# From a dense output product to a 32-expert mixture on one core: the router written anew, its neighbours put in another order

## The chip, the cores and the metric

The kernel runs on one core of one Trainium2 chip. A core has five engines that run side by side, each through its own list of instructions in order: TensorE (PE in the rows; PEld is its weight load), VectorE (DVE), ScalarE (ACT), GpSimd (POOL) and SyncE (SP). Here SP does nothing but issue DMAs, which 16 DMA engines carry out. An instruction waits, where it must, for semaphores of other engines, and everything behind it on its engine waits with it. SBUF is the on-chip memory of 128 partitions, PSUM the small memory into which TensorE writes. The metric is the device time of one execution in microseconds.

## The reference, cut to what matters

One decoder layer over 256 tokens of width 2048, in float32. Two token mixers run on the normalised input; they are merged, multiplied by `w_out` and added to `x`. Then comes the part that matters here:

```python
x = x + mixed @ w_out[l]
...
group_prob = softmax(ht @ wr_group + br_group)             # 4 groups
g_prob, g_idx = lax.top_k(group_prob, 1)
expert_logits = (ht @ wr_expert + br_expert).reshape(n_tok, N_GROUPS, EXPERTS_PER_GROUP)
sel = expert_logits[jnp.arange(n_tok), g_idx[:, 0]]        # the 8 experts of the token's group
top_logit, top_idx = lax.top_k(sel, TOP_K_INNER)           # its 2 best
weights = softmax(top_logit) * g_prob
for e in range(N_EXPERTS):                                 # 32
    hid = silu(ht @ w_gate[e]) * (ht @ w_up[e])
    out = out + gates[:, e:e + 1] * (hid @ w_down[e])
return rms_norm(x + out, norm_final_g)
```

Each expert's three matrices are 12 MiB, all 32 experts 384 MiB, read from HBM once.

## The kernel before, in words

**Stages.** The front end (input projection, the two mixers, their output products) is placed by a planner that has no part in the change. Behind it the code is written out in order: the product with `w_out` (four column blocks `n`, each in eight halves `kh` of two k-tiles, each weight half split into a high and a low part `wh`, `wl`); the router; the loop over 32 experts.

**Slots.** Large tiles of 1 MiB share 18 buffers; `slot(name)` takes one, `free(k)` counts k as given back, `room(k)` asks whether k are left. A buffer's next user waits for the last reader of its last tile. Through the `w_out` product the slots hold: 4 of `mix` (the activations), 2 of `acc` (the residual, addressed by `A`), 4 of `xn` (the normalised input, high and low part), one of `rt` (router weights and scratch), and 7 tiles of expert weights, issued earlier. When the front end's small pools close, four more buffers (`wx`) are there beside the slots (`wt`).

**The expert stream.** `Experts` (`xw`) hands out the 384 weight tiles in order: per expert 8 of gate and up (`mgu`), and 4 of down (`md`). `xw.issue` puts DMAs on SP while there is a buffer; `xw.done` gives back the tile just used and issues the next one, so from some point on a tile's DMA waits for the product that last read its buffer.

**Between the two.** `after(n, pss)` adds block `n` of the `w_out` product to `acc`, squares it for the norm, transposes it (PE, into PSUM), copies the transposes to `rt` (ACT), multiplies them with the router weights into `pl`, and splits the block into `xn`. Then `rr` is the reciprocal root of the mean square and `lg` the 36 logits of each token. The router (`first_max` three times) turns these into `asg`, a 0/1 matrix of tokens by experts; three small products with triangular matrices count the tokens of each expert (`pos`, a token's place among the 32 places of an expert). `gather(b)` makes from `pos` a one-hot `oh` for 8 experts and multiplies it with `xn` in eight steps of eight products; ACT copies each step's result to `xg`. `weights()` computes the gate values `gts`, `gtr`. `spread(q)` makes the one-hots `ohr` for four experts, the gate of each place (`gs`, by tiny products) and the transposed one-hots `ogT`.

**The first expert.** For e = 0 the loop takes one step of `gather(0)` before each of its eight steps `kt` of gate and up products (`gu`), then runs `spread(0)`, then `hd` (Silu on ACT, a product on DVE) and its transposes; then expert 1 begins. For e > 0 the steps follow each other as weights come in, and `down(e - 1)`, the scatter products and the later gathers stand between them.

Nearly all instructions are issued by one recording helper, so their line is L167; tiles tell them apart. L301 is the issue of an expert tile, L333 that of a half of the other weights.

## Time and profile before

| | |
|---|---|
| runs of the kernel before | 1785.33, 1789.11, 1793.22 us; median 1789.11 |
| the profiled execution | 1787.91 us device time, of which the span of its instructions is 1786.1 us |
| busy in the span | PE 81%, DVE 46%, ACT 31%, POOL 2% |
| DMA | 534 MB; 421 GB/s from 860 us on |
| where the stages lie | front end to 701 us, `w_out` to 798 us, router to 811 us, experts to the end |

Times in rows count from the start of the span. In rows of the timeline the columns are start, duration, engine (a q behind it: its queue, which issues DMAs), line, operation, out<-in tiles, shapes, number of instructions, and in brackets the idle time of the engine just before and what ended it. PEclk and the granted clock are shares of TensorE's full 2.4 GHz; 0.50 is 1.2 GHz.

### The profile page before, as it was taken

The numbers are of one execution on the slowest core, as the hardware profiler recorded it, in microseconds if no ns is written. First come the engines' busy times: TensorE is split into PE (matmuls) and PEld (weight loads), VectorE is DVE, ScalarE is ACT, GpSimd is POOL, SyncE is SP. The second block draws the span as 40 slices with busy tenths as digits, with TensorE's granted clock in tenths as the row PEclk, the third lists the DMA queues.
The fourth block names the chain that finished last, engine by engine and source line by source line (L and its number), as shares of the span: only waits on it lengthen the run. The fifth ranks groups of instructions, "written<-read, shape, count | busy, mean of one in ns | idle before, by whom it ended". The sixth has DMA issues, their size and how long they took to land.

```text
span 1786.1 us, 29643 instructions
## 1 busy us (share of the span) xinstructions
PE 1451.9 (81%) x12604; PEld 960.8 (54%) x12604; DVE 821.4 (46%) x1241; ACT 556.5 (31%) x919; POOL 33.6 (2%) x64
## 2 busy tenths in 40 slices
PE   7999999999999999996767776667676776676673
PEld 6989998888988999874323222223121332221120
DVE  6999998889944567442212121212121212121213
ACT  6668556666555344442001000011000110000002
POOL 0000000000100000000000000000000000000000
PEclk9999999999999999997978777798877888777766
DMA  6554463334635478538999999999999999999993
GB/s 232 180 163 133 147 209 107 118 105 158 190 117 177 152 254 331 176 125 330 414 421 421 420 421 421 421 420 421 421 421 421 421 420 421 421 421 420 420 421 149
DMA packets 94953, 534.09 MB, mean 299 GB/s; under 512 B 10528, under 2 KB 10544, under 8 KB 45024
## 3 DMA queue, kind: packets, MB, share of 16 engines
q1 hardware_dynamic: 91792, 522.49, 74.5%
q0 software_dynamic: 3024, 9.64, 1.8%
q8 instruction: 102, 1.67, 0.4%
q14 instruction: 35, 0.29, 0.0%
HBM read 526.82 MB, written 5.28 MB: 298 GB/s over the span
## 4 chain that ended last, share of the span: by engine, by line
DMA 49%; PE 40%; DVE 5%; ACT 3%; issue 2%; SPq 0%; DVEq 0%; ACTq 0%
PE mm L167 23%; DMA wt<-in_mgu_dram 21%; DMA wt<-in_md_dram 12%; DMA wx<-in_mgu_dram 11%; PE s L167 7%; PE sd L167 6%; DMA wx<-in_md_dram 3%; PE gu L167 2%; DVE wl L167 2%; DVE vring L167 1%; PE tr L167 1%; ACT wh L167 1%; PE y L167 1%; DMA x<-in_x_dram 1%; ACT ring L167 1%
## 5 line engine op out<-in xcount | busy, mean ns | idle before, releaser
L167 PE MATMUL mm<-hT,wh 128*128 128x256 f32 x2144 | 397.4, 287 | 5.7 <-ACT sg L167 3.0
L167 PEld LDWEIGHTS mm<-hT,wh 128*128 128x128 f32 x2144 | 330.1, 189 | 21.2 <-issue 9.9
L167 PE MATMUL gu<-wt,xg 128*32 128x256 f32 x2896 | 236.8, 457 | 102.8 <-DMA wt<-in_mgu_dram 94.5
L167 DVE TENSOR_TENSOR wl<-wr,wh 128x1024 fp32r<-128x1024 f32 x213 | 259.1, 1217 | 123.2 <-ACT wh L167 121.4
L167 PE MATMUL mm<-hT,wl 128*128 128x256 f32 x1072 | 302.7, 282 | 0.9 <-DVE wl L167 0.9
L167 ACT CAST wh<-wr 128x1024 fp32r<-128x1024 f32 x213 | 222.2, 1043 | 236.3 <-PE mm L167 150.2
L167 PEld LDWEIGHTS gu<-wt,xg 128*32 128x32 f32 x2896 | 88.8, 125 | 223.6 <-DMA wt<-in_mgu_dram 143.0
L167 PEld LDWEIGHTS mm<-hT,wl 128*128 128x128 f32 x1072 | 202.8, 189 | 1.5 <-DVE wl L167 1.3
L167 DVE TENSOR_TENSOR acc<-acc,sc 128x1024 f32<-128x1024 f32 x128 | 150.5, 1217 | 93.2 <-PE sc L167 93.2
L167 DVE SCALAR_TENSOR_TENSOR hd<-gu,gs,hd 64x256 f32<-64x256 f32 x32 | 15.7, 491 | 320.1 <-ACT hd L167 269.0
L167 DVE SCALAR_TENSOR_TENSOR ys<-y,gs,ys 128x512 fp32r<-128x512 f32 x32 | 24.0, 751 | 272.0 <-ACT ys L167 272.0
L167 PE MATMUL gu<-wx,xg 128*32 128x256 f32 x1200 | 104.7, 482 | 45.6 <-DMA wx<-in_mgu_dram 45.0
L167 ACT ACTIVATE ys<-y,gs 128x512 fp32r<-128x512 f32 x32 | 22.0, 687 | 280.0 <-PE y L167 280.0
L167 ACT ACTIVATE hd<-gu,gs 64x256 f32<-64x256 f32 x32 | 15.0, 468 | 259.5 <-PE gu L167 259.1
L167 PEld LDWEIGHTS gu<-wx,xg 128*32 128x32 f32 x1200 | 37.9, 130 | 99.5 <-DMA wx<-in_mgu_dram 68.7
L167 PE MATMUL sc<-ys,ogT 32*128 32x512 f32 x512 | 55.5, 509 | 28.8 <-DVE acc L167 27.7
L167 ACT ACTIVATE xg<-tr,prm 128x256 f32<-128x256 f32 x64 | 26.9, 471 | 161.2 <-PE tr L167 145.2
L167 ACT CAST ogT<-tr 128x256 fp32r<-128x256 f32 x32 | 11.8, 373 | 160.8 <-PE tr L167 160.7
L167 PEld LDWEIGHTS sc<-ys,ogT 32*128 32x128 f32 x512 | 23.6, 213 | 63.6 <-issue 43.6
L167 PEld LDWEIGHTS tr<-oh,xn 128*128 128x128 f32 x256 | 36.0, 209 | 15.5 <-issue 14.4
L167 PE MATMUL tr<-oh,xn 128*128 128x256 f32 x256 | 42.9, 315 | 1.0 <-DVE oh L167 1.0
L167 DVE TENSOR_TENSOR vring<-s,ring 128x512 f32<-128x512 f32 x64 | 42.4, 683 | 0.1
(462 smaller groups left out, 2042.4 us busy)
## 6 DMA issues: line engine op xcount, KB each, us to landing
wt<-in_mgu_dram SPq DMA_DIRECT2D x181, 1024.0 KB, 19.8
wt<-in_md_dram SPq DMA_DIRECT2D x87, 1024.0 KB, 19.8
wx<-in_mgu_dram SPq DMA_DIRECT2D x75, 1024.0 KB, 19.8
wr<-in_win_dram SPq DMA_DIRECT2D x132, 512.0 KB, 3.6
wx<-in_md_dram SPq DMA_DIRECT2D x41, 1024.0 KB, 19.8
wr<-in_wglu_dram SPq DMA_DIRECT2D x32, 512.0 KB, 3.8
wr<-in_wout_dram SPq DMA_DIRECT2D x32, 512.0 KB, 4.3
wr<-in_wro_dram SPq DMA_DIRECT2D x16, 512.0 KB, 6.7
```

The costliest lines, as they stand in the source:

```text
L167: return self._tl.do(Op(self._k, lambda: f(*a, **k), c, outs, ins, own, fn, name == "dma_start"))
```

## The change

Six things are done, in one edit.

- The router finds the two best experts in every group at once (tiles `x1`, `x2` of 4 by 8, with a new constant `io8`), beside the best group, and picks the group at the end; before, it took the group's logits out first.
- `pos` counts from 1, and is compared with 1 to 32, so that a subtraction falls away.
- The last block of `after` is changed: a dummy square root before it brings ACT's table earlier; one of the two copies to `rt` goes to DVE; the low part of `xn` is made behind the router. Silu's table is likewise asked for in `weights()`.
- Two steps of `gather(0)` come before the first expert's first step, so that each later step gathers one ahead; `spread(0)` makes its one-hots right behind `weights()`, and its products with the identity come after `hd` has been issued.
- The `mix` slots hold four k-tiles each in both parts; in the last block of `w_out` they are given back in two parts and a rest, and three expert tiles are issued in between.
- Six products of constants (`ident` with `iot`) follow the router's products on PE.

```diff
@@ -409,6 +409,8 @@
     pool.iota(jp, pattern=[[1, 128]], base=0, channel_multiplier=-1, allow_small_or_imprecise_dtypes=True)
     iot = cp.tile([128, T], F32, name="iot")
     pool.iota(iot, pattern=[[1, T]], base=0, channel_multiplier=0, allow_small_or_imprecise_dtypes=True)
+    io8 = cp.tile([128, 8, 8], F32, name="io8")
+    pool.iota(io8, pattern=[[0, 8], [1, 8]], base=0, channel_multiplier=0, allow_small_or_imprecise_dtypes=True)
     mask = cp.tile([128, 2, 128], F32, name="mask")
     dve.tensor_scalar(mask[:, 0], jp, 0.0, None, op0=OP.is_gt)
     dve.tensor_scalar(mask[:, 1], jp, 0.0, None, op0=OP.is_ge)
@@ -1177,8 +1179,8 @@
         yield
         while not room(4):
             yield "wait"
-        mh = [[slot("mix", F32R) for _ in range(2)] for _ in range(2)]
-        St["mix"] = lambda k: [t[k // 8][:, (k % 8) * T:(k % 8 + 1) * T] for t in mh]
+        mh = [slot("mix", F32R) for _ in range(4)]
+        St["mix"] = lambda k: [mh[k // 4][:, (k % 4 * 2 + x_) * T:(k % 4 * 2 + x_ + 1) * T] for x_ in range(2)]
         yk = [[t[:, k * T:(k + 1) * T] for t in Y] for k in range(8)]
         def put_mix(j, ps):
@@ -1252,6 +1254,9 @@
         xT = [rt[:, 576 + 512 * i:1088 + 512 * i] for i in range(2)]
         pts = [None, None]
+        if n == 3:
+            act.activation(cst[:, 5:6], cst[:, 0:1], AF.Sqrt)
         for i in range(2):
             a = A(i, n * 512)
             dve.tensor_add(a, a, pss[i])
@@ -1265,7 +1270,10 @@
                 pe.transpose(pts[i][:, j * 128:(j + 1) * 128], A(i, n * 512 + j * 128, 128), ident)
         yield
         for i in range(2):
-            act.copy(xT[i], pts[i])
+            if n == 3 and i == 0:
+                dve.tensor_copy(xT[i], pts[i])
+            else:
+                act.copy(xT[i], pts[i])
         yield
         for i in range(2):
             for j in range(4):
@@ -1274,7 +1282,10 @@
         yield
         for i in range(2):
             cs = slice(n * 512, (n + 1) * 512)
-            split(xn[i][0][:, cs], xn[i][1][:, cs], A(i, n * 512))
+            if n < 3:
+                split(xn[i][0][:, cs], xn[i][1][:, cs], A(i, n * 512))
+            else:
+                act.copy(xn[i][0][:, cs], A(i, n * 512))
     prev = iter(())
     for n in range(4):
@@ -1293,10 +1304,18 @@
                     for x_, y_ in ((0, 0), (0, 1), (1, 0)):
                         pe.matmul(pss[i], lhsT=a[x_], rhs=wk[y_], start=(k == 0 and x_ + y_ == 0),
                                   stop=(k == 15 and x_ == 1))
+            if n == 3 and kh in (3, 5, 7):
+                for _ in range(2 if kh == 3 else 1):
+                    free()
+                    xw.issue(xw.n + 1, 2 if kh == 7 else 0)
         prev = after(n, pss)
     for _ in range(4):
         next(prev)
-    free(4)
+    ps = psd()
+    for _ in range(6):
+        pe.matmul(ps[:, :T], lhsT=ident, rhs=iot, start=True, stop=True)
     rr = cp.tile([128, 2, 1], F32, name="rr")
     dve.tensor_reduce(rr, ssp, axis=AX.X, op=OP.add)
     act.activation(rr, rr, AF.Sqrt, bias=c_rms, scale=1.0 / D)
@@ -1325,50 +1344,49 @@
     R = lambda n, w: stile([128, 2] + list(w), "ro_" + n, 1)
     bc = lambda ap, *w: ap.to_broadcast([128, 2] + list(w))
-    def first_max(src, w, nm):
-
-        m = R(nm + "m", [1])
-        dve.tensor_reduce(m, src, axis=AX.X, op=OP.max)
-        eq = R(nm + "e", [w])
-        dve.tensor_tensor(eq, src, bc(m, w), op=OP.is_lt)
-
-        dve.scalar_tensor_tensor(eq, eq, 100.0, bc(iot[:, None, 0:w], w), op0=OP.mult, op1=OP.add)
-        ix = R(nm + "i", [1])
-        dve.tensor_reduce(ix, eq, axis=AX.X, op=OP.min)
-        oh = R(nm + "o", [w])
-        dve.tensor_tensor(oh, bc(iot[:, None, 0:w], w), bc(ix, w), op=OP.is_equal)
-        return m, oh
-
     l4 = lg[:, :, 0:4]
     l32 = lg[:, :, 4:36].rearrange("p i (g e) -> p i g e", g=4)
-    gm, goh = first_max(l4, 4, "g")
-    g48 = bc(goh[:, :, :, None], 4, 8)
+    i4, i48 = bc(iot[:, None, 0:4], 4), io8.rearrange("p (i g) e -> p i g e", i=2)
+    gm, m1, m2 = R("gm", [1]), R("m1", [4]), R("m2", [4])
+    xg_, x1, x2 = R("xg", [4]), R("x1", [4, 8]), R("x2", [4, 8])
+    gi, j1, j2 = R("gi", [1]), R("j1", [4]), R("j2", [4])
+    goh, oh1, oh2 = R("goh", [4]), R("oh1", [4, 8]), R("oh2", [4, 8])
+    e8 = lambda ap: bc(ap[:, :, :, None], 4, 8)
+    dve.tensor_reduce(m1, l32, axis=AX.X, op=OP.max)
+    dve.tensor_reduce(gm, l4, axis=AX.X, op=OP.max)
+    dve.tensor_tensor(x1, l32, e8(m1), op=OP.is_lt)
+    dve.tensor_tensor(xg_, l4, bc(gm, 4), op=OP.is_lt)
+    dve.scalar_tensor_tensor(x1, x1, 100.0, i48, op0=OP.mult, op1=OP.add)
+    dve.scalar_tensor_tensor(xg_, xg_, 100.0, i4, op0=OP.mult, op1=OP.add)
+    dve.tensor_reduce(j1, x1, axis=AX.X, op=OP.min)
+    dve.tensor_reduce(gi, xg_, axis=AX.X, op=OP.min)
+    dve.tensor_tensor(oh1, i48, e8(j1), op=OP.is_equal)
+    dve.tensor_tensor(goh, i4, bc(gi, 4), op=OP.is_equal)
+    sel2 = x1
+    dve.scalar_tensor_tensor(sel2, oh1, -1e30, l32, op0=OP.mult, op1=OP.add)
     ge = R("ge", [4])
     dve.tensor_sub(ge, l4, bc(gm, 4))
     act.activation(ge, ge, AF.Exp)
-    selp = R("selp", [4, 8])
-    dve.tensor_mul(selp, l32, g48)
-    sel = R("sel", [8])
-    dve.tensor_reduce(sel, selp.rearrange("p i g e -> p i e g"), axis=AX.X, op=OP.add)
-    m1, oh1 = first_max(sel, 8, "a")
-    sel2 = R("sel2", [8])
-    dve.scalar_tensor_tensor(sel2, oh1, -1e30, sel, op0=OP.mult, op1=OP.add)
-    m2, oh2 = first_max(sel2, 8, "b")
-    e2 = R("e2", [1])
-    dve.tensor_sub(e2, m2, m1)
-    act.activation(e2, e2, AF.Exp)
-    ohs = R("ohs", [8])
+    dve.tensor_reduce(m2, sel2, axis=AX.X, op=OP.max)
+    dve.tensor_tensor(x2, sel2, e8(m2), op=OP.is_lt)
+    dve.scalar_tensor_tensor(x2, x2, 100.0, i48, op0=OP.mult, op1=OP.add)
+    dve.tensor_reduce(j2, x2, axis=AX.X, op=OP.min)
+    dve.tensor_tensor(oh2, i48, e8(j2), op=OP.is_equal)
+    ohs = x2
     dve.tensor_add(ohs, oh1, oh2)
     asg = R("asg", [32])
-    dve.tensor_mul(asg.rearrange("p i (g e) -> p i g e", g=4), bc(ohs[:, :, None, :], 4, 8), g48)
+    dve.tensor_mul(asg.rearrange("p i (g e) -> p i g e", g=4), ohs, e8(goh))
     pp = pst("tr", 2)
     pe.matmul(pp[:, 0:32], lhsT=mask[:, 0], rhs=asg[:, 0], start=True, stop=True)
     pe.matmul(pp[:, 32:64], lhsT=onesm, rhs=asg[:, 0], start=True, stop=False)
     pe.matmul(pp[:, 32:64], lhsT=mask[:, 0], rhs=asg[:, 1], start=False, stop=True)
+    for i in range(2):
+        dve.tensor_tensor(xn[i][1][:, 1536:], A(i, 1536), xn[i][0].bitcast(F32)[:, 1536:], op=OP.subtract)
     pos = R("pos", [32])
     dve.scalar_tensor_tensor(pos, pp[:, 0:64].rearrange("p (i e) -> p i e", i=2), 1.0, asg, op0=OP.add, op1=OP.mult)
-    dve.tensor_scalar(pos, pos, 1.0, None, op0=OP.subtract)
     gts = R("gts", [32])
     gtr = R("gtr", [32, 2])
@@ -1376,6 +1394,14 @@
     def weights():
+        e4, e2 = R("e4", [4]), R("e2", [1])
+        dve.tensor_sub(e4, m2, m1)
+        dve.tensor_mul(e4, e4, goh)
+        dve.tensor_reduce(e2, e4, axis=AX.X, op=OP.add)
+        act.activation(e2, e2, AF.Exp)
+        act.activation(cst[:, 5:6], cst[:, 0:1], AF.Silu)
         gs = R("gs", [1])
         dve.tensor_reduce(gs, ge, axis=AX.X, op=OP.add)
         gp = R("gp", [1])
@@ -1386,16 +1412,16 @@
         dve.tensor_mul(w1, w1, gp)
         w2 = R("w2", [1])
         dve.tensor_mul(w2, w1, e2)
-        dve.tensor_mul(oh1, oh1, bc(w1, 8))
-        dve.tensor_mul(oh2, oh2, bc(w2, 8))
+        o8 = lambda o: o.rearrange("p i g e -> p i (g e)")
+        dve.tensor_mul(o8(oh1), o8(oh1), bc(w1, 32))
+        dve.tensor_mul(o8(oh2), o8(oh2), bc(w2, 32))
         dve.tensor_add(oh1, oh1, oh2)
-        dve.tensor_mul(gts.rearrange("p i (g e) -> p i g e", g=4), bc(oh1[:, :, None, :], 4, 8), g48)
+        dve.tensor_mul(gts.rearrange("p i (g e) -> p i g e", g=4), oh1, e8(goh))
         dve.tensor_copy(gtr[:, :, :, 0], gts)
         dve.tensor_copy(gtr[:, :, :, 1], bc(rr, 32))
-        ovf = R("ovf", [32])
-        dve.scalar_tensor_tensor(ovf, pos, float(CAP), gts, op0=OP.is_ge, op1=OP.mult)
-        ov1 = R("ov1", [32])
-        dve.tensor_scalar(ov1, pos, float(CAP), None, op0=OP.is_ge)
+        ovf, ov1 = (x_.rearrange("p i g e -> p i (g e)") for x_ in (x1, x2))
+        dve.scalar_tensor_tensor(ovf, pos, float(CAP + 1), gts, op0=OP.is_ge, op1=OP.mult)
+        dve.tensor_scalar(ov1, pos, float(CAP + 1), None, op0=OP.is_ge)
         ov2 = stile([128, 1], "ov2", 1)
         dve.tensor_reduce(ov2, ov1, axis=AX.XY, op=OP.max)
         pool.dma_start(ovd, ovf)
@@ -1416,7 +1442,7 @@
         oh = [stile([128, 8, CAP], "oh%d" % i, 1, F32R) for i in range(2)]
         for i in range(2):
             pb = pos[:, i, 8 * b:8 * b + 8][:, :, None].to_broadcast([128, 8, CAP])
-            dve.tensor_tensor(oh[i], iot[:, None, 0:CAP].to_broadcast([128, 8, CAP]), pb, op=OP.is_equal)
+            dve.tensor_tensor(oh[i], iot[:, None, 1:CAP + 1].to_broadcast([128, 8, CAP]), pb, op=OP.is_equal)
         G8[b] = xg
         yield
         for d2 in range(8):
@@ -1537,8 +1563,11 @@
             yield from spread(2 * b + 2)
     gq = gather(0)
-    next(gq)
+    for _ in range(2):
+        next(gq)
     ov2 = weights()
+    sp0 = spread(0)
+    next(sp0)
     hd_, hT_ = None, None
     at_e = [0]
     for e in range(NE + 1):
@@ -1570,7 +1599,7 @@
             gu = pst("gu", 1)
             for kt in range(8):
                 if e == 0:
-                    next(gq)
+                    next(gq, None)
                 w = xw.next()
                 for kk in range(2):
                     for c in range(4):
@@ -1582,10 +1611,7 @@
                 xw.done()
                 back()
             if e == 0:
-                for _ in gq:
-                    pass
-                for _ in spread(0):
-                    pass
+                next(sp0)
                 gq = beside(0)
             if e % 8 == 7:
                 for _ in gq:
@@ -1603,6 +1629,9 @@
             fin["sq"], fin["o"] = half("sq"), [slot("o") for _ in range(2)]
         if e:
             down(e - 1, hT_)
+        else:
+            for _ in sp0:
+                pass
         if e < NE:
             hps = pst("tr", 2)
             for j in range(2):
```

On SP, at the end of the `w_out` product (`wr` are its weight halves, `wx` and `wt` expert tiles), before:

```order
L333 DMA wr_8609<-in_wout_dram 128x2x512
L333 DMA wr_8637<-in_wout_dram 128x2x512
L301 DMA wx_8769<-in_mgu_dram 128x2048
L301 DMA wx_8771<-in_mgu_dram 128x2048
L301 DMA wx_8773<-in_mgu_dram 128x2048
L301 DMA wx_8775<-in_mgu_dram 128x2048
L301 DMA wt_8777<-in_mgu_dram 128x2048
L301 DMA wt_8779<-in_mgu_dram 128x2048
L301 DMA wt_8781<-in_mgu_dram 128x2048
L301 DMA wt_8890<-in_mgu_dram 128x2048
```

and of the change:

```order
L333 DMA wr_8611<-in_wout_dram 128x2x512
L333 DMA wr_8639<-in_wout_dram 128x2x512
L301 DMA wt_8659<-in_mgu_dram 128x2048
L301 DMA wt_8661<-in_mgu_dram 128x2048
L301 DMA wt_8707<-in_mgu_dram 128x2048
L301 DMA wx_8783<-in_mgu_dram 128x2048
L301 DMA wx_8785<-in_mgu_dram 128x2048
L301 DMA wx_8787<-in_mgu_dram 128x2048
L301 DMA wx_8789<-in_mgu_dram 128x2048
L301 DMA wt_8910<-in_mgu_dram 128x2048
```

Three `wt` tiles, which wait for reads of `mix`, now stand ahead of the four `wx` tiles, which wait for the last product with `w_out`; the number of tiles up to `wt_8890` and `wt_8910` is the same.

On PE, from the router's products to the second step of the first expert (`oh` and `xn` are the gather's operands, `gu` the expert's product), before:

```order
L167 MATMUL tr_8828<-ro_asg_8826,onesm_8783 128x32
...
L167 MATMUL tr_8871<-oh_687_8844,xn_8071 128x256
L167 MATMUL gu_8870<-wt_7497,xg_8841 32x256 x8
L167 MATMUL tr_8892<-oh_686_8843,xn_8068 128x256
...
L167 MATMUL tr_8892<-oh_687_8844,xn_8071 128x256
L167 MATMUL gu_8870<-wt_7572,xg_8841 32x256 x8
```

and of the change:

```order
L167 MATMUL sd_8758<-iot,ident 128x256 x6
L167 MATMUL tr_8827<-ro_asg_8825,mask 128x32
...
L167 MATMUL tr_8847<-oh_683_8844,xn_8073 128x256
L167 MATMUL tr_8891<-oh_682_8843,xn_8070 128x256
...
L167 MATMUL gu_8890<-wt_7499,xg_8841 32x256 x8
L167 MATMUL tr_8912<-oh_682_8843,xn_8070 128x256
...
L167 MATMUL gu_8890<-wt_7574,xg_8841 32x256 x8
```

Each `gu` now reads the gather before the one that stands just ahead of it.

On ACT, at the end of the first expert (`ogT` are the copies of `spread`, `hd` the Silu), before:

```order
L167 ACTIVATE xg_8842<-tr_9018,prm 128x256 x2
L167 CAST ogT_9044<-tr_9055 128x256
L167 CAST ogT_9044<-tr_9059 128x256
L167 CAST ogT_9044<-tr_9063 128x256
L167 CAST ogT_9044<-tr_9067 128x256
L167 ACT_TABLE_LOAD
L167 ACTIVATE hd_9071<-gu_8870,gs_9043 64x256
L167 COPY hT__722_9077<-tr_9074 128x128
```

and of the change:

```order
L167 ACTIVATE xg_8842<-tr_9017,prm 128x256 x2
L167 ACTIVATE hd_9060<-gu_8890,gs_9048 64x256
L167 CAST ogT_9049<-tr_9063 128x256
L167 CAST ogT_9049<-tr_9067 128x256
L167 CAST ogT_9049<-tr_9071 128x256
L167 CAST ogT_9049<-tr_9075 128x256
L167 COPY hT__719_9082<-tr_9079 128x128
```

The Silu stands ahead of the four copies, and the table load has gone to a place behind the first gather's copies.

## Rows read from the trace of the kernel before

**Rows 1.** The page, part 4: the chain that ended last, by engine.

```profile
DMA 49%; PE 40%; DVE 5%; ACT 3%; issue 2%; SPq 0%; DVEq 0%; ACTq 0%
```

**Rows 2.** Windows: stretch, length, busy time of five engines, PEclk, DMA share, GB/s.

```profile
783.50:799.00 15.50, 15.15 (x77) 12.46 (x75) 6.26 (x7) 4.92 (x9) 0.20 (x1) 1.00 0.00 1
804.30:817.80 13.50, 7.34 (x38) 5.51 (x38) 8.06 (x42) 1.76 (x6) 0.55 (x1) 0.50 1.02 425
838.50:848.50 10.00, 7.23 (x57) 4.00 (x61) 1.78 (x3) 3.42 (x7) 0.00 (x0) 0.50 0.37 145
860.00:1740.00 880.00, 613.11 (x5656) 222.46 (x5648) 188.06 (x205) 70.52 (x167) 1.01 (x2) 0.79 1.01 421
```

**Rows 3.** Timeline of SP's queue: last half of `w_out`, then expert tiles.

```profile
779.76 0.37 SPq L333 DMA_DIRECT2D wr<-in_wout_dram  x1
798.22 1.98 SPq L301 DMA_DIRECT2D wx<-in_mgu_dram  x4
845.37 0.33 SPq L301 DMA_DIRECT2D wx<-in_mgu_dram  x1
```

**Rows 4.** Timeline, from the end of `w_out` to the logits, three engines.

```profile
798.22 0.69 DVE L167 TENSOR_TENSOR acc<-acc,mm 128x512 f32<-128x512 f32 x1 [0.70 <-PE mm L167]
799.64 1.05 ACT L167 COPY rt<-sd 128x512 f32<-128x512 f32 x2
800.25 1.98 PE L167 MATMUL sd<-rt 128*128 128x36 f32 x16 [0.63 <-ACT rt L167]
800.71 1.28 ACT L167 ACT_TABLE_LOAD   x1
802.60 0.42 DVE L167 SCALAR_TENSOR_TENSOR lg<-sd,rr,rbt 128x36 f32<-128x36 f32 x2
802.93 1.28 DVE L167 TENSOR_TENSOR xn<-acc,xn 128x512 fp32r<-128x512 f32 x2
```

**Rows 5.** Timeline of DVE in the router.

```profile
804.13 0.15 DVE L167 TENSOR_REDUCE ro_gm<-lg 128x2 f32<-128x8 f32 x1
...
805.00 0.16 DVE L167 TENSOR_TENSOR ro_ge<-lg,ro_gm 128x8 f32<-128x8 f32 x1
805.12 0.22 DVE L167 TENSOR_TENSOR ro_selp<-lg,ro_go 128x64 f32<-128x64 f32 x1
805.38 0.27 DVE L167 TENSOR_REDUCE ro_sel<-ro_selp 128x16 f32<-128x64 f32 x1
805.68 0.17 DVE L167 TENSOR_REDUCE ro_am<-ro_sel 128x2 f32<-128x16 f32 x1
...
808.17 0.22 DVE L167 TENSOR_TENSOR ro_asg<-ro_ohs,ro_go 128x64 f32<-128x64 f32 x1
810.04 0.23 DVE L167 SCALAR_TENSOR_TENSOR ro_pos<-tr,ro_asg 128x64 f32<-128x64 f32 x1 [1.65 <-PE tr L167]
810.30 0.20 DVE L167 TENSOR_SCALAR ro_pos<-ro_pos 128x64 f32<-128x64 f32 x1
```

**Rows 6.** Timeline of PE in the first expert: first step, a later gather, last step.

```profile
811.01 2.07 PE L167 MATMUL tr<-oh,xn 128*128 128x256 f32 x8 [1.01 <-DVE oh L167]
814.00 1.94 PE L167 MATMUL gu<-wt,xg 128*32 128x256 f32 x16 [0.92 <-ACT xg L167]
...
819.51 1.21 PE L167 MATMUL tr<-oh,xn 128*128 128x256 f32 x8
...
835.15 1.07 PE L167 MATMUL gu<-wx,xg 128*32 128x256 f32 x16 [0.56 <-ACT xg L167]
```

**Rows 7.** Timeline of ACT and PE between the first expert and the second.

```profile
840.24 0.37 ACT L167 CAST ogT<-tr 128x256 fp32r<-128x256 f32 x1 [0.30 <-PE tr L167]
840.63 1.28 ACT L167 ACT_TABLE_LOAD   x1
841.92 0.47 ACT L167 ACTIVATE hd<-gu,gs 64x256 f32<-64x256 f32 x1
843.38 3.21 PE L167 MATMUL gu<-wx,xg 128*32 128x256 f32 x28
```

More of the change, by code (lines that the diff above doesn't have):

```diff
@@ L1440, in spread @@
             pb = pos[:, i, 4 * q:4 * q + 4][:, :, None, None].to_broadcast([128, 4, 4, CAP])
-            dve.tensor_tensor(oh[i], iot[:, None, None, 0:CAP].to_broadcast([128, 4, 4, CAP]), pb, op=OP.is_equal)
+            dve.tensor_tensor(oh[i], iot[:, None, None, 1:CAP + 1].to_broadcast([128, 4, 4, CAP]), pb, op=OP.is_equal)
         yield
```

## The prediction

> **What bounds the kernel now.** I read the page's chain by engine first. It splits the blame almost evenly, DMA 49% and PE 40% [rows 1], so two different limits follow each other, and the next question is where one hands over to the other. The windows answer it [rows 2]: from 860 to 1740 us the DMA share is 1.01 at 421 GB/s, so the expert stream fills the DMA engines without a pause. One tile of 1 MiB (1,048,576 bytes) takes 2.49 us at that rate. Nothing that PE, DVE or ACT do in that stretch can move the end; what moves it is when the stream gets going for good.
>
> It doesn't do so at once. Two windows ahead of 860 show holes. In 783.5 to 799 the share is 0.00: the last half of `w_out`'s weights is issued at 779.76, and the next DMA, the first expert tile after it, at 798.22 [rows 3]. From then on the stream runs (1.02 in the router's window), and stops again: in 838.5 to 848.5 the share is 0.37, so some 6.3 us of ten are empty [rows 2]. That second hole ends with SP's issue at 845.37 [rows 3]. All buffers were full; this issue waits until expert 2's first step has read its tile. PE starts that step at 843.38 with 28 products together [rows 7]; sixteen of them, one step, take 1.94 us at the low clock [rows 6], which ends at 845.32, and SP follows 0.05 later. So the length of the tail is fixed, and **the end follows that release one for one**. What precedes the release is one chain: end of `w_out` (798.22), logits (802.60), router (804.13 to 810.5), first expert (811.01 to 836.22), the gap to expert 2 (to 843.38) [rows 4 to 7].
>
> **What holds this to one for one.** The stream takes up the lead only if DMA has room. Part 5 of the change issues three tiles in `w_out`'s last block, into the first hole; this is 3 x 2.49 = 7.5 us of transfers taken away from behind 798. The total of buffers is unchanged, so the three don't let the stream run further ahead of PE; they only make the second hole begin 7.5 us earlier. It begins at about 840 to 841 now (3.7 us of the ten are busy; after the issue at 845.37 some 2.5 of them lie behind the hole, so 1.2 to 2.2 ahead of it), and would begin at about 833.2. A release earlier than that wins nothing more: the cap is 7.5 + about 5.3 = 12.8 us. Below it the release decides. The early tiles do not themselves shorten PE's path, and I put their own price at nothing: PE has no weight to wait for in the idle window (15.15 busy of 15.5 [rows 2]), and the last `w_out` half has been issued ahead of the three on SP's queue, so that it shares bandwidth with one of them at the most. Were that cover gone, one tile's 2.49 us would be the price.
>
> **Front of the router.** ACT loads a table (1.28) between its copies to `rt` and the square root, and `lg` is made at 802.60, 0.37 behind the end of PE's small products at 802.23 (800.25 + 1.98) [rows 4]. With the load earlier, and one of the two copies of 1.05 on DVE, the products can begin earlier by most of one copy, less its start behind DVE's own work. I take 0.8, between 0.4 (DVE's copy starts late) and 1.05 (one whole copy). The two `xn` differences of 1.28 in sum [rows 4] stand between `lg` and the router's first reduction; they go behind the three counting products, where DVE waits 1.65 for PE anyway [rows 5]. 803.02 to 804.13 is 1.11, so I take 1.1 (0.9 to 1.1; should the cover go, at most the 1.28 comes back in another place). The six constant products stand behind the logits' products on PE, whose next work waits for `asg`, ready today at 808.39 [rows 5] and by this sum near 806. PE has some 4 us there. Six products of 256 columns take 1.6 by the gather (eight in 2.07 [rows 6]) and 5.3 by the logits' products (16 of 36 columns in 1.98 [rows 4], scaled by columns). I take nothing as their cost, since the logits' products are small and mostly start-up, and keep 1.2 of loss as a bound.
>
> **The router's chain on DVE.** It runs from 804.13 to 808.39, 4.26 us for 22 instructions. The new order has 19, but thirteen work on 64 elements in place of 8 or 16. The rows price 64 wide at 0.22 to 0.27 where 8 and 16 wide are 0.15 to 0.17 [rows 5]. Nine at 0.26, four reductions at 0.30 and the six narrow ones at 0.15, largely hidden in between because they alternate with wide ones, give 3.5 to 4.4. I take a gain of 0.55; the bounds are a loss of 0.5 (all serial with wide ones at 0.30 and narrow at 0.16) and a gain of 0.7. The subtraction of `pos` (0.20 [rows 5]) falls away with its step: 0.2. `weights()` grows by some eight DVE instructions and one table load (1.28), but runs beside the first expert's 25 us on PE; ACT there does two short copies per step. `io8` is one more instruction on POOL long before.
>
> **The first expert.** Today g0 begins at 811.01 and the eighth `gu` ends at 835.15 + 1.07 = 836.22: 25.2 us [rows 6]. Each step is eight gather products, a wait for ACT's copy, and sixteen `gu`. At full clock these are 1.21 and 1.07, the wait 0.56; at half clock 2.07, 1.94 and 0.92 [rows 6]; PEclk is 0.50 up to 817.8 [rows 2]. Gathered one step ahead, each copy has a whole piece of PE work as cover, so the waits go: 8 x (1.21 + 1.07) = 18.2. One step at half clock adds 2.07 + 1.94 - 1.21 - 1.07 = 1.73. That makes 20.0, a gain of 5.2. The bounds: 3.5 with two such steps, 7.0 with none. I take one, because the constant products fill part of PE's pause, not all of it.
>
> **The gap to expert 2.** The last copy of `ogT` ends at 840.61; then ACT loads Silu's table (1.28), then comes `hd` (0.47), the product on DVE and the transposes, until `gu` of expert 2 at 843.38 [rows 7]. 2.77 us lie behind the last copy. Now Silu stands ahead of the copies and its table was fetched some 20 us sooner, so that load, Silu and product run beside `spread`'s products. At the least the load goes (1.28), at the most all 2.77; I take 2.4, as a few instructions still stand ahead of the first `gu`. A word on the price of a load: Silu starts at 841.92, right where the load's 1.28 ends [rows 7]; there is no further pause. The Trainium skill ("ScalarE: Activation LUTs", What ACT_TABLE_LOAD costs) counts a drain with it, some 2.66 us a switch; by that figure, an estimate, the moved load would be worth about 1.4 more. The sum goes by the row.
>
> **The sum.** 0.8 + 1.1 + 0.55 + 0.2 + 5.2 + 2.4 = 10.25 us, with bounds 0.4 + 0.9 - 1.2 - 0.5 + 0.2 + 3.5 + 1.28 = 4.6 and 1.05 + 1.1 + 0.7 + 0.2 + 7.0 + 2.77 = 12.8, right at the cap. The release would come at about 835.1, 1.9 behind the point where DMA runs dry, so it decides. Against the profiled execution, 1787.91 (1.8 around its span, 1.20 under the median of the runs), this is 1777.7; I say **1777.5 us**. The forecast's own range is 1775 to 1783.
>
> **The rivals.**
> *A, bytes.* Only the three early tiles count, because the release comes sooner than DMA can use it or the second hole stays: 7.5 us, 1780.4. For it: the holes are where the page shows them. Against: the hole's end is tied to SP's wait, not to bytes. Chance 0.09.
> *B, the clock, on the slower side.* All eight steps of the first expert run at 1.2 GHz: seven more than counted, 7 x 1.73 = 12.1 us, 1.9 more than the whole gain: 1789.8. It decides from about six such steps on. For it: in 838.5 to 848.5 the granted clock is 0.50 although PE is busy 7.23 of 10, and denser steps don't help if the clock fell in the router's wait [rows 2]. Against: with waits of 0.56 between its pieces, PE's gather at 819.51 already takes 1.21, and its last `gu` 1.07 [rows 6]. The Trainium skill ("TensorE: Matmul & The Clock Gate", HAM oscillation) says that waits between bursts of products bring the lower level back; by that rule the constants, followed by a wait for the router, would not keep the clock. Chance 0.07.
> *C, lost later.* The lead is eaten up in a later stall, or the stream's rate falls as denser PE work meets it: 1788. For it: PE is busy 613 of 880 us and not far from a bound when its clock is 0.79 [rows 2]. Against: share 1.01 throughout, no hole in which a stall shows. Chance 0.08.
>
> **How the numbers follow.** Forecast 0.76, A 0.09, B 0.07, C 0.08. A measurement of this kernel can tell about 0.5%, here 8.9 us. Of the forecast, 0.62 lies above a gain of 8.9 and 0.14 below; A is within, B and C are within for 0.09 together and beyond on the slow side for 0.06. So faster 0.62, same 0.32, slower 0.06. The range goes from 1770 (the cap, 1775.1, less the 3.8 us by which the fastest run of before lies under the median, and rounded down) to 1786, which takes in A and the terms' low ends, and leaves out B and C.
>
> **What would show it.** Right: SP's first issue for expert 2's release at 834 to 836 in place of 845.37; three expert tiles issued between 780 and 793 and a share above zero in 783.5 to 799; a hole of about 2 to 3 us in place of 6.3; gather steps without the 0.56 wait; Silu directly behind the last `gu`; 421 GB/s unchanged behind. Wrong: PEclk 0.50 beyond the first step (B); the second hole as long as before (A); a share under 1.00 in 860 to 1740 (C); a longer DVE stretch from the first reduction to `asg` than 4.26 (that term).

## The result and the profile after

Four runs of the changed kernel took 1772.50 to 1777.59 us, median 1775.13; four runs of the kernel before, beside them, 1785.33 to 1793.22, median 1788.28. The ratio is 0.9915, interval 0.9896 to 0.9934: 13 us faster. The profiled execution took 1777.59 us, its span 1775.8 (before 1786.1).

The chain by engine, on the page of the kernel after, hardly differs from [rows 1]:

```profile
DMA 48%; PE 40%; DVE 7%; ACT 2%; issue 2%; POOL 0%; SPq 0%; DVEq 0%; POOLq 0%; ACTq 0%
```

The difference is in the windows of the kernel after (columns as in [rows 2]):

```profile
783.50:799.00 15.50, 15.50 (x77) 12.91 (x76) 5.61 (x6) 6.64 (x9) 0.00 (x0) 1.00 0.64 216
804.30:817.80 13.50, 11.34 (x83) 8.35 (x83) 9.59 (x46) 5.97 (x13) 0.55 (x1) 0.87 0.96 384
...
828.00:838.00 10.00, 9.45 (x108) 5.87 (x96) 1.95 (x4) 2.13 (x6) 0.00 (x0) 0.83 0.98 371
838.50:848.50 10.00, 10.00 (x126) 5.12 (x129) 0.66 (x2) 1.82 (x5) 0.00 (x0) 1.00 1.01 397
860.00:1740.00 880.00, 607.76 (x5534) 220.81 (x5526) 182.62 (x201) 69.87 (x164) 1.01 (x2) 0.79 1.01 420
```

Both holes are smaller. Ahead of 799 the DMA share is 0.64 in place of 0.00. The 1.01 in place of 0.37 at 838.5 to 848.5 does not say this of the second hole by itself, since the release now lies ten us further ahead; but the stretch around it, 828 to 838, has a share of 0.98 at 371 GB/s. Measured by arrivals, two tiles land 4.30 apart there in place of the 2.49 of a full stream: 1.8 us are lost, where the kernel before loses 7.3 (9.77 apart). The stream behind runs at the same 420 GB/s. SP's queue, to set beside [rows 3]:

```profile
783.36 12.65 SPq L301 DMA_DIRECT2D wt<-in_mgu_dram  x3
801.26 2.01 SPq L301 DMA_DIRECT2D wx<-in_mgu_dram  x4
...
835.00 0.33 SPq L301 DMA_DIRECT2D wt<-in_mgu_dram  x1
```

The three early tiles stand in the first row; the third is issued at 795.68, 2.7 behind the forecast's 793. The issue that waits for expert 2's first step is at 835.00, where it was at 845.37: 10.37 earlier, and the span is 10.3 shorter. Yet the four `wx` tiles, issued as `w_out` ends, are 3.04 later than before. So what lies between the end of `w_out` and the release shrank by 13.4 us, and 3 were lost ahead of it, in the front end (see c1_after and the last section). The timeline of that stretch, to set beside [rows 4 to 7]:

```profile
801.26 0.69 DVE L167 TENSOR_TENSOR acc<-acc,mm 128x512 f32<-128x512 f32 x1 [0.70 <-PE mm L167]
...
801.87 0.68 DVE L167 COPY rt<-sd 128x512 f32<-128x512 f32 x1
...
802.61 1.98 PE L167 MATMUL sd<-rt 128*128 128x36 f32 x16
...
804.41 2.84 PE L167 MATMUL sd<-iot,ident 128*128 128x256 f32 x12
804.62 0.42 DVE L167 SCALAR_TENSOR_TENSOR lg<-sd,rr,rbt 128x36 f32<-128x36 f32 x2 [0.84 <-PE sd L167]
...
805.07 0.22 DVE L167 TENSOR_REDUCE ro_m<-lg 128x8 f32<-128x64 f32 x1
805.21 0.15 DVE L167 TENSOR_REDUCE ro_gm<-lg 128x2 f32<-128x8 f32 x1
805.33 0.22 DVE L167 TENSOR_TENSOR ro_x<-lg,ro_m 128x64 f32<-128x64 f32 x1
...
806.87 0.23 DVE L167 TENSOR_TENSOR ro_x<-ro_x,ro_m 128x64 f32<-128x64 f32 x1
807.13 0.22 DVE L167 SCALAR_TENSOR_TENSOR ro_x<-ro_x,io 128x64 f32<-128x64 f32 x1
...
808.16 0.23 DVE L167 TENSOR_TENSOR ro_asg<-ro_x,ro_goh 128x64 f32<-128x64 f32 x1
808.30 1.28 DVE L167 TENSOR_TENSOR xn<-acc,xn 128x512 fp32r<-128x512 f32 x2
...
808.53 0.38 PE L167 MATMUL tr<-ro_asg,mask 128*128 128x32 f32 x2 [1.28 <-DVE ro_asg L167]
...
809.50 0.22 DVE L167 SCALAR_TENSOR_TENSOR ro_pos<-tr,ro_asg 128x64 f32<-128x64 f32 x1
...
810.24 2.78 PE L167 MATMUL tr<-oh,xn 128*128 128x256 f32 x16 [0.88 <-DVE oh L167]
...
812.88 1.28 ACT L167 ACT_TABLE_LOAD   x1
...
812.94 1.94 PE L167 MATMUL gu<-wt,xg 128*32 128x256 f32 x16
...
814.17 0.20 ACT L167 ACTIVATE cst<-cst 128x1 f32<-128x1 f32 x1
...
816.07 1.07 PE L167 MATMUL gu<-wt,xg 128*32 128x256 f32 x16
...
818.20 1.07 PE L167 MATMUL gu<-wt,xg 128*32 128x256 f32 x16
...
826.74 1.93 PE L167 MATMUL gu<-wt,xg 128*32 128x256 f32 x32
...
830.78 0.47 ACT L167 ACTIVATE hd<-gu,gs 64x256 f32<-64x256 f32 x1 [3.10 <-DVE gs L167]
831.28 0.65 ACT L167 CAST ogT<-tr 128x256 fp32r<-128x256 f32 x2
...
833.01 3.18 PE L167 MATMUL gu<-wt,xg 128*32 128x256 f32 x32
```

Read it from its first row, the end of `w_out` (801.26), as zero. The router's first reduction starts at 3.81, 0.03 behind the logits (before: at 5.91, 1.11 behind them [rows 4, 5]). The low part of `xn` now lies exactly where DVE waited for the counting products. From 816 on no `gu` has a wait behind a gather. Silu stands ahead of the `ogT` copies and has no table load before it; it waits for the gates (`gs`) instead, which I hadn't foreseen. Silu's table is loaded at 812.88, beside PE's work, and the dummy Silu starts as the 1.28 end: as in [rows 7], the trace has nothing of the further pause that the Trainium skill ("ScalarE: Activation LUTs", What ACT_TABLE_LOAD costs) counts.

### The profile page after: what moved, and what is told of

Its sections match the earlier page's. It is cut to its first block, busy times and chain, and to the rows that moved or that the text cites. A ratio compares the mean times of both kernels' runs of the same rounds, so it can differ in the third digit from the quotient of the medians.

```text
span 1775.8 us, 29679 instructions
## 1 busy us (share of the span) xinstructions
PE 1454.9 (82%) x12616; PEld 967.9 (55%) x12616; DVE 821.4 (46%) x1241; ACT 555.8 (31%) x920; POOL 33.8 (2%) x65
## 4 chain that ended last, share of the span: by engine, by line
DMA 48%; PE 40%; DVE 7%; ACT 2%; issue 2%; POOL 0%; SPq 0%; DVEq 0%; POOLq 0%; ACTq 0%
DMA wt<-in_mgu_dram 24%; PE mm L167 22%; DMA wx<-in_md_dram 10%; DMA wx<-in_mgu_dram 9%; PE s L167 7%; PE sd L167 6%; DMA wt<-in_md_dram 5%; PE gu L167 2%; DVE wl L167 2%; DVE vring L167 1%; PE tr L167 1%; PE sc L167 1%; DVE vb L167 1%; ACT wh L167 1%; DMA x<-in_x_dram 1%
## 5 line engine op out<-in xcount | busy, mean ns | idle before, releaser
L167 PE MATMUL gu<-wt,xg 128*32 128x256 f32 x2944 | 245.6, 465 | 100.5 <-DMA wt<-in_mgu_dram 96.2
L167 PE MATMUL gu<-wx,xg 128*32 128x256 f32 x1152 | 96.8, 470 | 41.8 <-DMA wx<-in_mgu_dram 41.8
L167 PE MATMUL sc<-ys,ogT 32*128 32x512 f32 x512 | 60.7, 552 | 25.7 <-DVE acc L167 24.5
```

What stands on the lines that cost most here:

```text
L167: return self._tl.do(Op(self._k, lambda: f(*a, **k), c, outs, ins, own, fn, name == "dma_start"))
```

## The experiments

Eleven kernels were run beside the kernel before. Names with a are the change with one thing undone, except a_dense, which gives PE more to do; d_noearly is a_dense without the early tiles; names with b are the kernel before with one thing added; c1_after is the change again. The profiles are compared from the end of `w_out` (the start of its last addition to `acc`), which removes what happens ahead of it. "Release" is SP's first issue behind expert 2's first product, "last landing" the arrival of the 384th expert tile; both are from the trace's records, in us behind the end of `w_out`. In the ratio, the kernel before is 1, measured beside each kernel in its own set of runs (medians 1788.2 to 1789.4), so times are compared by it sooner than by the medians. There is one profile of each kernel.

| kernel | median us | ratio and interval | release | last landing | difference |
|---|---|---|---|---|---|
| before | 1788.3 | | 47.15 | 959.23 | 912.1 |
| after | 1775.13 | 0.9915 (0.9896 to 0.9934) | 33.74 | 946.99 | 913.3 |
| c1_after | 1772.91 | 0.9916 (0.9897 to 0.9935) | 33.97 | 946.31 | 912.3 |
| a_gather1 | 1782.10 | 0.9956 (0.9939 to 0.9974) | 42.64 | 954.82 | 912.2 |
| a_gap | 1775.40 | 0.9914 (0.9893 to 0.9935) | 36.32 | 947.59 | 911.3 |
| a_chain | 1778.57 | 0.9931 (0.9904 to 0.9958) | 33.53 | 946.71 | 913.2 |
| a_nodummy | 1776.21 | 0.9935 (0.9913 to 0.9957) | 34.54 | 947.86 | 913.3 |
| a_front | 1776.68 | 0.9942 (0.9923 to 0.9961) | 36.94 | 949.03 | 912.1 |
| b_gather | 1780.44 | 0.9960 (0.9944 to 0.9975) | 39.64 | 951.13 | 911.5 |
| b_early | 1788.46 | 1.0003 (0.9986 to 1.0020) | 46.76 | 958.71 | 912.0 |
| a_dense | 1772.55 | 0.9914 (0.9890 to 0.9938) | 31.23 | 944.26 | 913.0 |
| a_noearly | 1778.28 | 0.9949 (0.9931 to 0.9967) | 31.56 | 948.53 | 917.0 |
| d_noearly | 1776.94 | 0.9942 (0.9926 to 0.9958) | 31.23 | 950.06 | 918.8 |

The last column is the finding. Over a range of 16 us of release it stays at 911.3 to 913.3: to within these 2 us, the last landing follows the release one for one. It breaks in two kernels only, those that release early without the early tiles. A little is lost in the others too: the five that release before 35 stand at 912.3 to 913.3, the six later ones at 911.3 to 912.2, and the change, 13.4 ahead at the release, is 12.2 ahead at the last landing. Behind that come the last products and the output, 25.5 to 29.5 us in the thirteen profiles and in no order by the release (28.7 in before and in a_dense), so that the end itself moves by some us besides.

**The change again.**

> The changed kernel itself, unedited, as the yardstick of this set. Its first profile had SP's release by expert 2's first step at 835.00, 33.7 us behind the end of w_out (801.26), and its front end ended 3.0 us later than that of before. If those 3.0 us belong to the change, w_out ends near 801 here again; if they are chance, it may end near 798. The median should lie within 3 us of 1775.1.

`w_out` ended at 797.86, 0.36 ahead of the kernel before's 798.22, and the median was 1772.91: the 3 us ahead of it are not the change's.

**Early tiles: taken out of the change, and put alone into the kernel before.**

```diff
-            if n == 3 and kh in (3, 5, 7):
-                for _ in range(2 if kh == 3 else 1):
-                    free()
-                    xw.issue(xw.n + 1, 2 if kh == 7 else 0)
...
     for _ in range(4):
         next(prev)
+    free(4)
```

> The change without its three early expert tiles (all four buffers are given back behind w_out, as before). Release theory: the end follows expert 2's first step one for one until DMA is full. The release stays 33.7 us behind the end of w_out, but DMA now has 3 x 2.49 = 7.5 us more to carry behind it and had only about 1.8 us of room at the release (two landings 4.3 us apart in place of 2.5), so it becomes the limit: 4 to 6 us slower than the change, 1779 to 1781. Rival, release alone (DMA never limits): no change, 1775. Rival, bytes: 7.5 slower, 1782.6.

> The kernel before with nothing but the new mix buffers and the three early tiles. Release theory: PE reaches expert 2 no sooner, the hole ahead of it only begins 7.5 us earlier and is that much longer; the time stays within 2 us of before, about 1788. Rival, bytes: 7.5 us faster, about 1781.

Alone, the tiles give nothing (1.0003). The windows of b_early show it:

```profile
783.50:799.00 15.50, 15.50 (x76) 12.91 (x76) 5.54 (x6) 5.16 (x7) 0.00 (x0) 1.00 0.61 221
...
804.00:830.00 26.00, 16.07 (x134) 11.02 (x134) 9.75 (x48) 6.92 (x16) 0.55 (x1) 0.74 0.71 282
830.00:850.00 20.00, 15.54 (x149) 9.57 (x151) 1.96 (x4) 6.03 (x13) 0.00 (x0) 0.74 0.66 251
```

The first hole is filled to 0.61, and what is won there is idled away behind 804 (shares 0.71 and 0.66), as the stream waits for the same release. Taken out of the change they cost 5.4 us in the medians, though the intervals of the ratios overlap by a hair at 0.993; in the profiles the release came 2.2 to 2.4 earlier than in the change (PE kept its full clock through the first expert there; whether by chance or for want of the tiles, one profile can't tell) and the last landing still 1.5 to 2.2 later. That asked for the same release with and without them, which d_noearly gives below.

**The first gather one step ahead: undone, and put alone into the kernel before.**

```diff
-    for _ in range(2):
-        next(gq)
+    next(gq)
```

> The change with its first gather one step ahead undone: each gu waits again for ACT's copy of the step just before it. Release theory: seven or eight waits of 0.4 to 0.9 come back, the release lies 38 to 40 us behind the end of w_out in place of 33.7 to 34.0, and the last landing and the end move by the same 4 to 6 us: 1777 to 1779. Rival, DMA is the limit in the change already (its hole at the release is only 1.8 to 2.2 us): less than 2 us slower, under 1775.

> The kernel before with nothing but its first gather one step ahead. PE theory: by the undoing of it (release 8.8 later), the release comes 6 to 8.5 earlier behind the end of w_out than 47.15. Cap theory: without the early tiles DMA can use only about the length of its hole, some 5 to 7 us, so the last landing (959.2 behind w_out) moves by less than the release if that moves by over 6, and the end with it: 1781.5 to 1784. Rival, release alone: the landing moves by the whole of the release, up to 8.5, 1780.

The undoing cost more than was expected: 8.7 to 8.9 at the release, and some 7 us in the time by the ratios (0.9956 against 0.9915, intervals apart). PE's timeline in a_gather1:

```profile
807.26 1.57 PE L167 MATMUL tr<-oh,xn 128*128 128x256 f32 x8 [0.88 <-DVE oh L167]
810.18 1.94 PE L167 MATMUL gu<-wt,xg 128*32 128x256 f32 x16 [1.35 <-ACT xg L167]
812.04 2.08 PE L167 MATMUL tr<-oh,xn 128*128 128x256 f32 x8
...
819.13 1.07 PE L167 MATMUL gu<-wt,xg 128*32 128x256 f32 x16 [0.56 <-ACT xg L167]
```

The waits come back (1.35, then 0.56 each), and with them half clock up to the third gather: 2.08 and 1.94 where the change has 1.20 and 1.07 from its second `gu` on. Put alone into the kernel before, the step moved the release by 7.5 and the last landing by 8.1. The cap that I expected there, 5 to 7, did not show: the release's rival reading held.

**The gap, the chain on DVE, the end of `w_out`, the constants: each undone.**

```diff
-        act.activation(cst[:, 5:6], cst[:, 0:1], AF.Silu)
...
-                next(sp0)
+                for _ in sp0:
+                    pass
...
-        else:
-            for _ in sp0:
-                pass
```

> The change with the gap to expert 2 as before: spread's products and copies ahead of the first expert's Silu, whose table is loaded there. Release theory: from the last gu to expert 2's first product 7.2 us in place of 4.4 to 4.6, so the release 2.5 to 2.9 later behind the end of w_out, the end as much: about 1775.6. Rival: the load and Silu were beside PE work anyway, no change, 1773.

From the last `gu` to expert 2's first product it was 6.9 in place of 4.3 to 4.6, and the release 2.4 to 2.6 later; the last landing moved only 0.6 to 1.3, and the medians' intervals cover each other. Right at the release, within what the times can't tell.

```diff
-    dve.tensor_reduce(m1, l32, axis=AX.X, op=OP.max)
...
+    gm, goh = first_max(l4, 4, "g")
+    g48 = bc(goh[:, :, :, None], 4, 8)
...
+    m1, oh1 = first_max(sel, 8, "a")
...
+    m2, oh2 = first_max(sel2, 8, "b")
```

> The change with the old chain of 22 instructions on DVE from the logits to asg (group first, then its eight logits), all else as in the change. From the first reduction to asg 4.26 us in place of 3.32, so the release 0.9 later, the end 0.9 later, 1773.9: below what the medians can tell, so it is read from the trace. Rival, by my own bounds (64-wide instructions are dearer): no difference, or the old chain 0.5 faster.

From the first reduction to `asg` it took 4.27 in place of 3.31, the 0.95 of the expectation. At the release none of it was left (33.53). The first expert and the gap took 18.3 and 4.2, in the change 18.4 and 4.3; and, the larger part, expert 2 began at full clock here:

```profile
838.29 1.93 PE L167 MATMUL gu<-wt,xg 128*32 128x256 f32 x32
```

These are the products that take 3.18 in the change (833.01), and from their start to the release it is 1.13 in place of 1.99. The term is right as a stretch and too small to be seen behind the clock's play.

```diff
-        if n == 3:
-            act.activation(cst[:, 5:6], cst[:, 0:1], AF.Sqrt)
...
-            if n == 3 and i == 0:
-                dve.tensor_copy(xT[i], pts[i])
-            else:
-                act.copy(xT[i], pts[i])
+            act.copy(xT[i], pts[i])
...
-    for i in range(2):
-        dve.tensor_tensor(xn[i][1][:, 1536:], A(i, 1536), xn[i][0].bitcast(F32)[:, 1536:], op=OP.subtract)
```

> The change with the end of w_out's last block as before: no early square root, both copies to rt on ACT, the low part of xn made ahead of the router. From the end of w_out to the router's first reduction 5.9 us in place of 3.8, so the release 2.1 later (35.8 to 36.1) and the last landing 2.1 later, about 1775: read from the trace. Rival: PE's wait for asg grows, the clock falls lower for longer, and it is 3 to 4 us. Rival, DMA-limited: less than 1.

The router's first reduction came at 5.91, the 2.1; the release 3.0 to 3.2 later. The rest is the clock, as the rival said; PE in a_front:

```profile
808.52 0.60 PE L167 MATMUL tr<-ro_asg,mask 128*128 128x32 f32 x2 [2.69 <-DVE ro_asg L167]
...
810.75 3.79 PE L167 MATMUL tr<-oh,xn 128*128 128x256 f32 x16 [0.78 <-DVE oh L167]
```

PE waits 2.69 for `asg` (1.28 in the change), and the two gathers take 3.79 (2.78 in the change).

```diff
-    ps = psd()
-    for _ in range(6):
-        pe.matmul(ps[:, :T], lhsT=ident, rhs=iot, start=True, stop=True)
```

> The change without the six products of constants. If they hold the clock: the granted clock falls in the router's wait, the counting products and the first two gather steps run at half clock (2.07 in place of 1.21 to 1.39 each) and one more gu (1.94 in place of 1.07), 2 to 3.5 us later at the release, and the end 2 to 3.5 us later, 1777 to 1779. Rival: the clock falls all the same in the wait behind them, so that they do nothing: release 33.7 us behind w_out, 1775.

The release came only 0.6 to 0.8 later, of which 0.53 lies between `asg` and `pos`. Neither theory's number was met. Against the change's two profiles the six constants are worth less than a microsecond; against a_noearly, which has them too and kept its full clock, the release is 3.0 later. So what they are worth hangs on whether the clock then holds, and that these profiles leave open.

**Denser on PE.** Eight constants in place of six, two more behind the counting products, and parts of `spread(0)` among the first expert's steps:

```diff
-    for _ in range(6):
+    for _ in range(8):
...
+    pf = pst("gu", 1)
+    for _ in range(2):
+        pe.matmul(pf[:, 0:256], lhsT=ident, rhs=iot, start=True, stop=True)
...
+                if e == 0 and kt in (4, 5, 6):
+                    next(sp0)
...
-                next(sp0)
                 gq = beside(0)
```

> The change made denser on PE: eight products of constants in place of six, two more behind the counting products, and three parts of spread(0) (the gates' products and two of four expert transposes) among the first expert's steps. Expected: PE keeps full clock longer, Silu need not wait for the gates, so the release lies 1 to 2.5 us earlier behind the end of w_out (31.3 to 32.9); DMA's hole there (1.8 to 2.2) closes, the last landing comes 1 to 2 us earlier, and more could not be won: 1771 to 1772.5. Rival: the clock falls by chance and not by the idle time, the release does not move.

> The denser variant without the three early tiles. Release as in the denser variant, 31.2 behind the end of w_out. Cap theory: DMA decides, the last landing lies 948.0 to 949.0 behind w_out, as without early tiles in the change itself, 4 us or so behind the denser variant's 944.3: about 1777. Rival, release alone: 944.3, 1772.5.

PE's timeline of a_dense shows what it does:

```profile
805.16 1.11 PE L167 MATMUL gu<-iot,ident 128*128 128x256 f32 x4
806.21 2.25 PE L167 MATMUL tr<-oh,xn 128*128 128x256 f32 x16
808.43 1.07 PE L167 MATMUL gu<-wt,xg 128*32 128x256 f32 x16
...
818.16 1.95 PE L167 MATMUL tr<-ro_gtr,ohr 128*128 128x2 f32 x16
```

The first gathers and the first `gu` run at full clock (2.25 for two gathers and 1.07, where the change has 2.78 and 1.94), the gates' products no longer stand between the last `gu` and Silu, and the release is 2.5 to 2.7 earlier, the last landing 2.1 to 2.7. Windows of a_dense, and then of the kernel after, over the router and the first expert:

```profile
804.00:830.00 26.00, 24.84 (x281) 17.30 (x284) 8.35 (x31) 10.21 (x25) 0.54 (x1) 1.00 0.97 375
```

```profile
804.00:830.00 26.00, 23.84 (x229) 16.92 (x228) 9.59 (x46) 10.47 (x24) 0.55 (x1) 0.93 0.95 367
```

The granted clock is 1.00 in the one and 0.93 in the other. The Trainium skill ("TensorE: Matmul & The Clock Gate", HAM oscillation) says that waits between bursts of products bring the lower level back; with the waits filled, in a_dense and in d_noearly, the traces agree. But the rival, chance, is not ruled out. PE in a_noearly, where no more is filled than in the change:

```profile
807.64 0.38 PE L167 MATMUL tr<-ro_asg,mask 128*128 128x32 f32 x2 [1.28 <-DVE ro_asg L167]
...
809.35 2.23 PE L167 MATMUL tr<-oh,xn 128*128 128x256 f32 x16 [0.88 <-DVE oh L167]
811.57 1.07 PE L167 MATMUL gu<-wt,xg 128*32 128x256 f32 x16
```

It has the change's waits of 1.28 and 0.88, yet both gathers and the first `gu` run at full clock, and its release, 31.56, is only 0.3 behind a_dense's. After, c1_after and a_gap, with the same waits, take 2.78, 3.58 and 3.54 for the two gathers. So the earlier release goes with the full clock; that the filling is what keeps it is not shown. The median of a_dense, 1772.55, is not to be told from the change's; by the trace it is the earliest of all. Without the early tiles, with the very same release of 31.23, the last landing is 5.8 later and the median 4.4 (5.0 by the ratios, whose intervals still overlap). The windows of d_noearly say why:

```profile
783.50:799.00 15.50, 15.41 (x77) 12.64 (x75) 6.06 (x7) 6.69 (x11) 0.20 (x1) 1.00 0.00 1
...
804.00:830.00 26.00, 24.84 (x263) 17.37 (x265) 9.45 (x36) 10.53 (x27) 0.54 (x1) 1.00 1.01 422
830.00:850.00 20.00, 18.82 (x254) 9.83 (x250) 6.11 (x7) 2.58 (x7) 0.00 (x0) 1.00 1.01 420
```

From 804 on DMA is full without a break: here it is the limit, not the release.

## Why the prediction was right, step by step

**The mechanism held.** The last landing follows the release one for one to within 2 us, and the stream takes up any lead while DMA has room. Rival A (bytes alone) falls with b_early; rival B (all steps at half clock) with the 1.07 of the `gu` at 816.07; rival C with the 420 GB/s and 1.01 of the last window.

**The release came at 835.00, the forecast was 835.1; part of that is luck.** The terms, as the profile of after has them against before:

| term | forecast us | measured us |
|---|---|---|
| end of `w_out` to first reduction (0.8 + 1.1) | 1.9 | 2.10 |
| DVE chain to `asg` | 0.55 | 0.95 |
| `asg` to first gather | 0.2 | 0.77 |
| first expert | 5.2 | 6.78 |
| gap to expert 2 | 2.4 | 2.81 |
| sum | 10.25 | 13.4 |

Each term has the right sign and each is too small, by 3.2 in all; the profiled execution lost 3.04 ahead of it. The mis-sized steps: for the **first expert** I added whole durations, 1.21 + 1.07 = 2.28 a step, but the rows overlap, and the steps at full clock start 2.13 apart (816.07, 818.20): 8 x 0.15 = 1.2 of the 1.6 missing. Of the half-clock step of 1.73 some 1.4 was there (two gathers 2.78 in place of 2.40, one `gu` 1.94 in place of 1.07, and 0.12 on the next gather). For the **DVE chain** I let 64-wide and narrow instructions add up; in the new order a pair of a wide and a narrow one advances the chain by 0.26 (805.07 to 805.33), as a wide one alone does later (806.87 to 807.13), so the narrow ones cost nothing here, and the gain went beyond its bound of 0.7. (The bound on the other side, a loss of 0.5, comes to 0.6 by its own prices.) **From `asg` to the gather** I counted only the subtraction; the counting products also ran at full clock, which the run without the constants puts at 0.53. The constants themselves cost nothing, as forecast: they end at 807.25, and PE waits for `asg` until 808.53.

**The cap was sized wrongly.** I gave the hole 5.3 us; between the landings around it the stream of the kernel before loses 7.3, and b_gather moved the last landing by 8.1 without the early tiles. With the early tiles' 7.5 that makes a cap of 14.8 in place of 12.8, and the denser variant, with no hole left at its release (2.42 between two landings), reached a lead of 15.0. That a cap there is, the other two show: without the early tiles the last landing doesn't come before 948.5 to 950.1. In the change itself the early tiles were needed and not sufficient, as forecast; that they "do not themselves shorten PE's path" is what b_early shows.

**Where the 13 us came from,** then: about 7 to 9 from the gather ahead, some 3 from the end of `w_out`, 2.5 from the gap, under 1 from the constants, and from the chain 0.95 as a stretch and nothing at the release; and 4 to 6 of it kept only thanks to the early tiles (4.4 and 5.4 in medians, 5.8 in landings at one release). The parts measured one by one overlap, since each also moves the clock.

## What to carry to other kernels

When a stream saturates to the end, find the one wait from which it runs for good, and count every gain and loss up to that wait; up to the last landing the rest adds nearly a constant (911 to 913 us here), as long as DMA has room. A transfer moved into idle DMA time was worth nothing here until the work that frees its buffers also came sooner, and that work was worth only part until the bytes were moved: measure each alone and both together. Work whose result goes through another engine wants to be one step ahead; here, put alone into the kernel before, that was worth its waits (0.92 and seven of 0.56, 4.8 us) and 2.7 more at the release, in the clock and in products that overlap again.

## What the hardware showed that I had not expected

The time of the front end, where the change edits next to nothing (`io8` and the layout of the `mix` buffers), moves by chance, through TensorE's clock. Windows of c1_after and then of b_gather, the same stretch of the front end:

```profile
340.00:380.00 40.00, 39.51 (x282) 29.59 (x281) 31.59 (x50) 25.60 (x40) 0.56 (x1) 1.00 0.27 93
```

```profile
340.00:380.00 40.00, 39.51 (x233) 29.39 (x232) 25.58 (x42) 22.40 (x38) 0.57 (x1) 0.79 0.22 72
```

PE is busy 39.51 of 40 us in both, and the granted clock is 1.00 in the one and 0.79 in the other. Over the thirteen profiles, those with no such dip between 350 and 420 us end `w_out` at 797.2 to 798.5, those with a dip near 410 alone at 799.2 to 801.3 (that of the change's first profile among them), and those with one near 358 at 805.6 to 807.5. The dips come in the kernel before's front end as in the change's; what sets them off, no run here shows. What they move is as large as most of the terms above, which is why these were read from the end of `w_out`.
